# Interleaving loads and stores in one DMA ring, with a one-instruction row mean

## Chip, cores and metric

One core of a Trainium2 chip. The metric is the device time of one execution in microseconds (us); lower is better. Each version runs several times beside the kernel before on the same chip; medians are quoted. A ratio is computed as the mean time of one kernel's fast runs over the mean of the other's fast runs of the same rounds, so it isn't quite the ratio of the medians. "Same" means within 2%.

The profile knows these engines: DVE is VectorE, ACT ScalarE, POOL GpSimd and SP the engine that issues the transfers here. "DMA engines" are the 16 that move data. Besides the printed views I used the trace's packet records: one for each piece of a transfer (one partition's contiguous bytes) with its start and length. The records don't name the engine: figures per engine are sums divided by 16, or follow from one packet's end meeting the next one's start.

The "ring" is the queue's list of issued transfers. A transfer is "issued" when the instruction that queues it runs, and has "landed" when the profile reports it complete. Nearly all packets of one size took the same time: 2418 ns for 64 KiB (382 of 384 in the kernel before, within 1%), 1966 for 52 and 1815 for 48 (126 of 128 and 226 of 256 in the first profile of the changed kernel), 460 for 12 (all 128 in a3). Such packets are called undisturbed.

## The reference

```python
def reference(x, axis):           # x: 1024 x 4096 float32, axis = -1
    mean = np.mean(x, axis=axis, keepdims=True)
    return ((x - mean) ** 2).astype(np.float32)
```

16.78 MB in, 16.78 MB out. Each of the 128 partitions holds eight rows of 16 KiB.

## The kernel before

Two tiles of four rows each. All loads are issued at once, on one queue; each tile is stored when all its rows are done. Means are split between VectorE (rows 0 to 2) and ScalarE (row 3); ScalarE squares all but the last 1792 columns of row 2, which VectorE squares.

```python
for i in range(ntiles):                       # ntiles = 2, Q = 4 rows per tile
    x_tile = io.tile([P, Q * D], F32)
    cuts = [0, HEAD, Q * D] if i == 0 else [0, Q * D]      # HEAD = 512
    for lo, hi in zip(cuts, cuts[1:]):
        nc.sync.dma_start(out=x_tile[:, lo:hi], in_=x_t[i][:, lo:hi])
# ... cut: helpers for mean and square ...
for i in range(ntiles):
    row = [tiles[i][:, q * D:(q + 1) * D] for q in range(Q)]
    m3 = mean_on_act(row[3])
    m0 = mean_on_dve(row[0])
    square_on_act(row[3], m3)
    # ... cut: rows 1 and 2 alike, the end of row 2 squared on VectorE ...
    nc.sync.dma_start(out=out_t[i], in_=tiles[i])
```

Of the kernel before, what the change touches and what calls it, by code (L numbers as in the profile page):

```python
# [2 lines left out]

os.environ.setdefault("NEURON_RT_ULTRASERVER_MODE", "4")

# [4 lines left out]

F32 = mybir.dt.float32
ACT = mybir.ActivationFunctionType


@with_exitstack
def kernel(
    ctx: ExitStack,
    tc: tile.TileContext,
    x: bass.AP,
    axis: bass.AP,  # L20
    out: bass.AP,
):





    nc = tc.nc

    B, D = x.shape  # L30
    P = nc.NUM_PARTITIONS
    Q = 4
    HEAD = 512
    H = D * 9 // 16
    assert B % (P * Q) == 0
    ntiles = B // (P * Q)
    inv_d = 1.0 / float(D)

    x_t = x.rearrange("(p n q) d -> n p (q d)", p=P, q=Q)
    out_t = out.rearrange("(p n q) d -> n p (q d)", p=P, q=Q)  # L40

    io = ctx.enter_context(tc.tile_pool(name="io", bufs=ntiles))
    scratch = ctx.enter_context(tc.tile_pool(name="scratch", bufs=1))
    stats = ctx.enter_context(tc.tile_pool(name="stats", bufs=2 * ntiles * Q))

    tiles = []
    for i in range(ntiles):
        x_tile = io.tile([P, Q * D], F32)
        cuts = [0, HEAD, Q * D] if i == 0 else [0, Q * D]
        for lo, hi in zip(cuts, cuts[1:]):  # L50
            nc.sync.dma_start(out=x_tile[:, lo:hi], in_=x_t[i][:, lo:hi])  # L51
        tiles.append(x_tile)

    inorder = tc.keep_in_program_order

    def mean_on_act(row):
        copy = scratch.tile([P, D], F32)
        neg_mean = stats.tile([P, 1], F32)
        nc.scalar.activation(  # L59
            out=copy, in_=row, func=ACT.Identity, scale=-inv_d, accum_out=neg_mean  # L60
        )
        return neg_mean

    def mean_on_dve(row):
        neg_sum = stats.tile([P, 1], F32)
        neg_mean = stats.tile([P, 1], F32)
        inorder(nc.vector.reduce_sum(  # L67
            out=neg_sum, in_=row, axis=mybir.AxisListType.X, negate=True
        ))
        inorder(nc.vector.tensor_scalar_mul(out=neg_mean, in0=neg_sum, scalar1=inv_d))  # L70
        return neg_mean

    def square_on_act(part, neg_mean):
        inorder(nc.scalar.activation(  # L74
            out=part, in_=part, func=ACT.Square, bias=neg_mean, scale=1.0
        ))

    for i in range(ntiles):
        row = [tiles[i][:, q * D:(q + 1) * D] for q in range(Q)]
        m3 = mean_on_act(row[3])  # L80
        m0 = mean_on_dve(row[0])
        square_on_act(row[3], m3)
        m1 = mean_on_dve(row[1])
        square_on_act(row[0], m0)
        m2 = mean_on_dve(row[2])
        square_on_act(row[1], m1)
        square_on_act(row[2][:, :H], m2)
        back = row[2][:, H:]
        nc.vector.tensor_scalar_add(out=back, in0=back, scalar1=m2)  # L89
        nc.vector.tensor_mul(out=back, in0=back, in1=back)  # L90
        nc.sync.dma_start(out=out_t[i], in_=tiles[i])


# [1 line left out]
_INS = ['x', 'axis']  # L95
_OUTS = [((1024, 4096), 'float32')]

_NUMBERS = {'axis': -1}


# [26 lines left out]
```

## Time and profile before

| kernel before | |
|---|---|
| time, 6 runs | 83.28 us median (83.11 to 84.35) |
| span in the profile | 81.4 us |
| VectorE, ScalarE busy | 33.4, 34.7 us |
| DMA queue busy, as share of 16 engines | 95.9% |
| first store issued | 39.56 us |
| last load packets end, by engine (packet records) | 40.8 to 41.6 us |

A digit in the rows by slice is the busy share of one fortieth of the span, in tenths. The prediction below shows the lines of the engines, the queue, the compute groups and the stores. One more line matters later, from the list of DMA issues of the kernel before. Its last column is the time from issue to landing:

```profile
x_tile<-in_x_dram SPq DMA_DIRECT2D x1, 40.2
```

This is the second load, issued near 1.6 us behind the others and landed at 41.9.

### The profile page before, as it was taken

Reading aid. Unit: us, or ns where it says so; the run is one execution under the profiler, and the core shown is the slowest. Engines: PE = TensorE matmul, PEld = TensorE weight load, DVE = VectorE, ACT = ScalarE, POOL = GpSimd, SP = SyncE. Lnnn points to the kernel's source line nnn. Section 1 sums busy time; section 2 is a strip of 40 time slices with the busy share of each in tenths; the row PEclk is TensorE's granted clock in tenths of the full one; section 3 lists DMA queues with packets and bytes.
Section 4 is the critical chain, followed back from the end, with each engine's and each line's share of the span. In section 5 each row is a group of like instructions: output and inputs, shape, how many; then the busy total and the mean of one; then the engine's idle time right before and its main releaser. Section 6 shows DMA issues by size and latency. Waiting matters only on the chain.

```text
span 81.4 us, 83 instructions
## 1 busy us (share of the span) xinstructions
DVE 33.4 (41%) x16; ACT 34.7 (43%) x13; POOL 0.2 (0%) x4
## 2 busy tenths in 40 slices
DVE  0000000000089999999439999999900000000000
ACT  6000000000099999999339999999800000000000
POOL 0000000000000000000000000000000000000000
DMA  1999939999992999993899998399999199999290
GB/s 26 602 499 468 406 156 468 499 499 499 516 451 97 483 516 516 516 483 161 387 516 516 516 483 387 161 516 516 516 516 451 64 516 516 516 516 483 129 419 0
DMA packets 720, 33.55 MB, mean 412 GB/s; under 512 B 80, under 2 KB 80, under 8 KB 208
## 3 DMA queue, kind: packets, MB, share of 16 engines
q1 hardware_dynamic: 720, 33.55, 95.9%
HBM read 16.78 MB, written 16.78 MB: 412 GB/s over the span
## 4 chain that ended last, share of the span: by engine, by line
DMA 49%; DVE 21%; SPq 1%; issue 0%
DMA x_tile<-in_x_dram 49%; DVE neg_sum L67 16%; DVE x_tile L90 2%; DVE x_tile L89 1%; SPq L51 1%; DVE neg_mean L70 1%
## 5 line engine op out<-in xcount | busy, mean ns | idle before, releaser
L67 DVE TENSOR_REDUCE neg_sum<-x_tile 128x1 f32<-128x4096 f32 x6 | 26.5, 4412 | 25.0 <-DMA x_tile<-in_x_dram 25.0
L74 ACT ACTIVATE x_tile<-x_tile,neg_mean 128x4096 f32<-128x4096 f32 (+1 forms) x8 | 26.0, 3324 | 0.1
L59 ACT ACTIVATE copy<-x_tile 128x4096 f32<-128x4096 f32 x2 | 7.2, 3617 | 23.1 <-DMA x_tile<-in_x_dram 23.1
L90 DVE TENSOR_TENSOR x_tile<-x_tile 128x1792 f32<-128x1792 f32 x2 | 4.1, 2026 | 0.1
L89 DVE TENSOR_SCALAR x_tile<-x_tile,neg_mean 128x1792 f32<-128x1792 f32 x2 | 2.3, 1153 | 0.1
L59 ACT ACT_TABLE_LOAD x1 | 1.3, 1283 | 0.7 <-PEq L108 0.7
L70 DVE TENSOR_SCALAR neg_mean<-neg_sum 128x1 f32<-128x1 f32 x6 | 0.9, 154 | 0.2
L59 ACT ACTIVATION_READ_ACCUMULATOR copy<-x_tile 128x1 f32 x2 | 0.4, 186 | 0.0
L108 POOL MEMSET const-bfloat16-1.0<- 128x1 bf16 x1 | 0.1, 102 | 0.0
L108 POOL MEMSET const-uint8-127<- 128x1 uint8 x1 | 0.1, 101 | 0.0
L108 POOL MEMSET const-float32-0.0<- 128x1 f32 x1 | 0.1, 99 | 0.2 <-issue 0.2
L108 POOL MEMSET const-float32-1.0<- 128x1 f32 x1 | 0.1, 98 | 0.0
## 6 DMA issues: line engine op xcount, KB each, us to landing
x_tile<-in_x_dram SPq DMA_DIRECT2D x1, 7936.0 KB, 21.4
x_tile<-in_x_dram SPq DMA_DIRECT2D x1, 256.0 KB, 2.6
out_dram<-x_tile SPq DMA_DIRECT2D x2, 21.7
x_tile<-in_x_dram SPq DMA_DIRECT2D x1, 40.2
```

The lines of the kernel that those rows point to most:

```text
L51: nc.sync.dma_start(out=x_tile[:, lo:hi], in_=x_t[i][:, lo:hi])
L59: nc.scalar.activation(out=copy, in_=row, func=ACT.Identity, scale=-inv_d, accum_out=neg_mean)
L67: inorder(nc.vector.reduce_sum(out=neg_sum, in_=row, axis=mybir.AxisListType.X, negate=True))
L70: inorder(nc.vector.tensor_scalar_mul(out=neg_mean, in0=neg_sum, scalar1=inv_d))
L74: inorder(nc.scalar.activation(out=part, in_=part, func=ACT.Square, bias=neg_mean, scale=1.0))
L89: nc.vector.tensor_scalar_add(out=back, in0=back, scalar1=m2)
L90: nc.vector.tensor_mul(out=back, in0=back, in1=back)
L108: nc = _bacc.Bacc("TRN2", target_bir_lowering=False, num_devices=1)
```

## The change

Its intent: put the first store into the ring before the last piece of the loads, so that the ring alternates and results leave earlier, and cut compute with one VectorE instruction that adds a row's two halves, scales and sums them.

```diff
-    for i in range(ntiles):
-        x_tile = io.tile([P, Q * D], F32)
-        cuts = [0, HEAD, Q * D] if i == 0 else [0, Q * D]
-        ...
+    data = io.tile([P, ROWS * D], F32)
 ...
-        inorder(nc.vector.reduce_sum(
-            out=neg_sum, in_=row, axis=mybir.AxisListType.X, negate=True
-        ))
-        inorder(nc.vector.tensor_scalar_mul(out=neg_mean, in0=neg_sum, scalar1=inv_d))
+        inorder(nc.vector.tensor_tensor_reduce(
+            out=pairs, in0=row[:, :HALF], in1=row[:, HALF:],
+            scale=-inv_d, scalar=0.0, op0=ADD, op1=ADD, accum_out=neg_mean,
+        ))
 ...
+    load(0, 512)
+    load(512, 4 * D)
+    load(4 * D, 8 * D - 3 * D // 4)
+    for r in range(3):
+        compute(r)
+    store(0, 2)
+    load(8 * D - 3 * D // 4, 8 * D)
+    for r in range(3, 6):
+        compute(r)
+    store(3, 5)
+    for r in range(6, 8):
+        compute(r)
+    store(6, 7)
```

`load(lo, hi)` and `store(first, last)` are transfers on the same queue, in program order; `compute(r)` is the mean on VectorE and the whole square on ScalarE.

More of the change, by code (lines that the diff above doesn't have):

```diff
@@ L12 @@
 ACT = mybir.ActivationFunctionType
+ADD = mybir.AluOpType.add
 @with_exitstack
@@ L31 @@
     P = nc.NUM_PARTITIONS
-    Q = 4
-    HEAD = 512
-    H = D * 9 // 16
-    assert B % (P * Q) == 0
-    ntiles = B // (P * Q)
+    ROWS = B // P
+    HALF = D // 2
+    assert B == P * ROWS and ROWS == 8
     inv_d = 1.0 / float(D)
-    x_t = x.rearrange("(p n q) d -> n p (q d)", p=P, q=Q)
-    out_t = out.rearrange("(p n q) d -> n p (q d)", p=P, q=Q)
-    io = ctx.enter_context(tc.tile_pool(name="io", bufs=ntiles))
+    x_t = x.rearrange("(p r) d -> p (r d)", p=P)
+    out_t = out.rearrange("(p r) d -> p (r d)", p=P)
@@ L43 @@
+    io = ctx.enter_context(tc.tile_pool(name="io", bufs=1))
     scratch = ctx.enter_context(tc.tile_pool(name="scratch", bufs=1))
-    stats = ctx.enter_context(tc.tile_pool(name="stats", bufs=2 * ntiles * Q))
-    tiles = []
-    for i in range(ntiles):
-        x_tile = io.tile([P, Q * D], F32)
-        cuts = [0, HEAD, Q * D] if i == 0 else [0, Q * D]
-        for lo, hi in zip(cuts, cuts[1:]):
-            nc.sync.dma_start(out=x_tile[:, lo:hi], in_=x_t[i][:, lo:hi])
-        tiles.append(x_tile)
@@ L54 @@
-    inorder = tc.keep_in_program_order
-    def mean_on_act(row):
-        copy = scratch.tile([P, D], F32)
-        neg_mean = stats.tile([P, 1], F32)
-        nc.scalar.activation(
-            out=copy, in_=row, func=ACT.Identity, scale=-inv_d, accum_out=neg_mean
-        )
-        return neg_mean
-    def mean_on_dve(row):
-        neg_sum = stats.tile([P, 1], F32)
-        neg_mean = stats.tile([P, 1], F32)
-        inorder(nc.vector.reduce_sum(
-            out=neg_sum, in_=row, axis=mybir.AxisListType.X, negate=True
-        ))
-        inorder(nc.vector.tensor_scalar_mul(out=neg_mean, in0=neg_sum, scalar1=inv_d))
-        return neg_mean
@@ L73, in square_on_act, with load, store, compute @@
-    def square_on_act(part, neg_mean):
+    stats = ctx.enter_context(tc.tile_pool(name="stats", bufs=ROWS))
+    data = io.tile([P, ROWS * D], F32)
+    inorder = tc.keep_in_program_order
+    def load(lo, hi):
+        inorder(nc.sync.dma_start(out=data[:, lo:hi], in_=x_t[:, lo:hi]))
+    def store(first, last):
+        part = slice(first * D, (last + 1) * D)
+        inorder(nc.sync.dma_start(out=out_t[:, part], in_=data[:, part]))
+    def compute(r):
+        row = data[:, r * D:(r + 1) * D]
+        pairs = scratch.tile([P, HALF], F32)
+        neg_mean = stats.tile([P, 1], F32)
+        inorder(nc.vector.tensor_tensor_reduce(
+            out=pairs,
+            in0=row[:, :HALF],
+            in1=row[:, HALF:],
+            scale=-inv_d,
+            scalar=0.0,
+            op0=ADD,
+            op1=ADD,
+            accum_out=neg_mean,
+        ))
@@ L74, in square_on_act @@
         inorder(nc.scalar.activation(
-            out=part, in_=part, func=ACT.Square, bias=neg_mean, scale=1.0
+            out=row, in_=row, func=ACT.Square, bias=neg_mean, scale=1.0
         ))
-    for i in range(ntiles):
-        row = [tiles[i][:, q * D:(q + 1) * D] for q in range(Q)]
-        m3 = mean_on_act(row[3])
-        m0 = mean_on_dve(row[0])
-        square_on_act(row[3], m3)
-        m1 = mean_on_dve(row[1])
-        square_on_act(row[0], m0)
-        m2 = mean_on_dve(row[2])
-        square_on_act(row[1], m1)
-        square_on_act(row[2][:, :H], m2)
-        back = row[2][:, H:]
-        nc.vector.tensor_scalar_add(out=back, in0=back, scalar1=m2)
-        nc.vector.tensor_mul(out=back, in0=back, in1=back)
-        nc.sync.dma_start(out=out_t[i], in_=tiles[i])
+    load(0, 512)
```

## The prediction

> **What bounds the kernel now.** I read the page from the top. Its first two parts say that no compute engine is the limit and that the transfers are:
>
> ```profile
> DVE 33.4 (41%) x16; ACT 34.7 (43%) x13; POOL 0.2 (0%) x4
> ...
> DMA  1999939999992999993899998399999199999290
> ...
> q1 hardware_dynamic: 720, 33.55, 95.9%
> HBM read 16.78 MB, written 16.78 MB: 412 GB/s over the span
> ```
>
> VectorE and ScalarE work for about 40% of 81.4 us. The one DMA queue keeps all 16 DMA engines busy for 95.9% of the span, 78.1 us. The work in those 78.1 us is fixed by the reference: 33.55 MB, 2,097,152 bytes for each engine, so 2,097,152 / 78.1 us = 26.9 bytes per ns and engine. The isolated low digits in the DMA row come from how whole packets of 2.4 us fall into slices of 2.0 us: in the packet records of the trace each engine starts the next packet within some 5 to 10 ns of the one before, from the first packet at 1.74 us to the last end at 80.22 us. What is left of the span is 1.74 us ahead (the first issue at 0.73, a further 1.0 us until its first packet) and 1.1 us behind.
>
> The chain of work that ended last names DMA for only half of the span and then VectorE:
>
> ```profile
> 1.64 40.24 DMA x_tile<-in_x_dram
> ...
> 55.57 1.16 DVE x_tile L89
> ...
> 56.76 2.02 DVE x_tile L90
> ```
>
> This chain stops at 58.8 us, where the second store is issued, and does not follow it through the queue. It would mislead: shortening VectorE's part would only put that store into the ring sooner, behind a store that isn't done. The queue's own waits and the issues show this:
>
> ```profile
> 39.56 19.64 SPq L91 DMA_DIRECT2D out_dram<-x_tile  x2
> ...
> out_dram<-x_tile SPq DMA_DIRECT2D x2, 21.7
> ```
>
> Store 1 is issued at 39.56 us while the second load lands at 41.88 us; store 2 is issued at 58.9 us (39.56 + 19.64 less its own 0.35), store 1 lands at 39.56 + 21.7 = 61.3 us. Both stores are queued about 2.3 us before the ring reaches them, so no compute time is exposed at all. **The bound is one ring that is never empty**, and its length is bytes over rate.
>
> [...] a 65,536-byte packet took 2.418 us, 27.1 bytes per ns, times 16 is 433.7 GB/s. [...] on the single queue the packets of store 1 start at 41 us, when the load's end, although it was issued at 39.56. So the change can put work in another order in this ring but can't get it through sooner. [...]
>
> **The change part by part.**
>
> *Bytes.* The same 33.55 MB, one queue. Nothing to gain: 2,097,152 / 27.1 = 77.4 us per engine before and after.
>
> *Mean and square.* Away go six reductions of 4412 ns, six small scalings of 154 ns, two ScalarE means of 3617 ns and the two VectorE squares:
>
> ```profile
> L67 DVE TENSOR_REDUCE neg_sum<-x_tile 128x1 f32<-128x4096 f32 x6 | 26.5, 4412 | 25.0 <-DMA x_tile<-in_x_dram 25.0
> L59 ACT ACTIVATE copy<-x_tile 128x4096 f32<-128x4096 f32 x2 | 7.2, 3617 | 23.1 <-DMA x_tile<-in_x_dram 23.1
> L90 DVE TENSOR_TENSOR x_tile<-x_tile 128x1792 f32<-128x1792 f32 x2 | 4.1, 2026 | 0.1
> L89 DVE TENSOR_SCALAR x_tile<-x_tile,neg_mean 128x1792 f32<-128x1792 f32 x2 | 2.3, 1153 | 0.1
> L70 DVE TENSOR_SCALAR neg_mean<-neg_sum 128x1 f32<-128x1 f32 x6 | 0.9, 154 | 0.2
> ```
>
> In their place come eight add-and-sum instructions over two halves of 2048 columns. An estimate from L90: [...] about 0.1 us to write the sum out (ScalarE's accumulator read took 186 ns), so 2.4 us. VectorE then works 8 x 2.4 = 19 us instead of 33.4. ScalarE does eight full squares of 3.7 us, 29.6 us instead of 34.7. All of this lies beside the ring; by itself it is worth nothing.
>
> *When the first store reaches the ring.* Here the change can cost something. The two first loads are as before, so row 0 starts at 22.61 us as L67 did. Its mean ends at 25.0; three squares follow on ScalarE, which the trace shows starting 3.60 us apart (four, one of them 2.20 us long, took 13.01), so 2 x 3.60 + 3.70 = 10.9 and the last ends at 25.07 + 10.9 = 35.97. Issue at 36.03 us (L91 was issued 0.06 us after VectorE's end). First packet 1.0 us later, as at the start: 37.04 us. The third load is now 52 KiB per partition: the engines began it between 21.5 and 22.2 us, and eight packets of 53,248 / 27.1 = 1.965 us end at 37.2 to 37.9 us. The store comes **0.2 us ahead of the first engine that runs dry, 0.9 ahead of the last**. It should fit, but before the margin was 2.3 - 1.0 = 1.3 us; now it is nearly gone.
>
> *Later issues.* Store of rows 0 to 2: eight packets of 48 KiB per engine, 14.5 us, to about 52; the last 12 KiB, 3.6 us, to 55.7. Rows 4 and 5 land near 38.3, their squares end near 48.2: store of rows 3 to 5 is issued 7 us before it is needed. Row 7 lands near 56.4, takes 2.4 + 3.7, so the last store is issued near 62.7, while the one ahead runs to 70. Both hidden.
>
> *Ring overhead.* The ring has 7 transfers instead of 5, that is 56 instead of 40 packets per engine; a 2 KiB packet took 81 ns at best against 75.6 by rate, so about 5 ns each: 0.08 us. It changes direction three times (load to store, store to load, load to store) instead of once. Before, the packets after the switch began 2.49 to 2.62 us after the ones ahead, normally 2.41: 0.1 to 0.2 us per switch. Two more: about 0.2 us, partly taken up by slack between engines (they finish 0.54 us apart).
>
> *Sum:* 83.23 + 0.08 + about 0.1 = **83.4 us**, a change of 0.2%.
>
> **Rivals.** (1) *The add-and-sum runs at half rate*[...]: 4.3 + 0.1 us a row. The first mean ends 2.1 us later; ScalarE still follows 3.7 us behind, VectorE's pace of 4.4 now sets the third square: 22.61 + 3 x 4.4 + 3.7 + 0.1 = 39.6, first packet 40.6. The ring stands empty for 2.7 to 3.4 us and the time is about 86.3. [...] I give it 6%. (2) *A small hole at the first store*: a fixed cost of 0.3 to 0.8 us more in the new instruction, or a slower issue, empties the ring by about as much: 83.6 to 84.2. The 0.2 us margin speaks for it; I give it 30%. (3) *Less VectorE and ScalarE work shows as time*: the chain suggests VectorE's 21% matter. It would make 80 or less. Against it: both stores already wait in the ring; bytes at 433.7 GB/s leave only the ends of the span, 2.9 us, and the change touches neither. 1%. (4) *The mix of directions lets reads and writes overlap in the engines* and runs above 27.1 bytes per ns: the packets of both directions take the same 2.418 us[...]. 1%, about 82.
>
> **Range and chances.** The centre is 83.4. The low end, 83.0, is the run-to-run scatter below 83.2; the high end, 84.3, holds a hole of 0.9 us. Over 2% slower means above 84.9, a hole of 1.5 us or more: rival 1 and a bad case of rival 2, together 7%. Over 2% faster, below 81.6, needs rival 3 or more than rival 4: 1%. The rest, 92%, is the same.
>
> **What would show it.** In the changed profile: one queue at 95 to 96% of the span again, with 33.55 MB; VectorE near 19 us and ScalarE near 31 us with its table load; the add-and-sum near 2.3 us in the groups (4.4 would mean rival 1); the first store issued near 36.0 us; the DMA row near 37 us without a hole wider than a slice's scatter; stores 2 and 3 issued about 7 us before the ring comes to them. The prediction is wrong if the first store is issued after 37 us, if any later store is issued to an empty ring, if the switches of direction cost over 0.5 us each, or if the custom add-and-sum brings a start-up that holds back the first load.

## The result

The changed kernel took 84.48 us (median of 6, 84.03 to 87.23) against 83.28. The ratio of fast runs is 1.013, 95% interval 1.0098 to 1.0162. That is within 2%, as forecast, but above the predicted range of 83.0 to 84.3, and clear of noise. Two of the six runs were slow (87.23 and 85.36 us); the four fast ones took 84.03 to 84.52, with a median of 84.29, at the range's upper edge. Executions over 1.5% slower than the fastest of the same kernel are left out of the means.

The profile taken with it fell in a slow run (87.23 us), where in the packet records one DMA engine of the 16 ran about 1.5 us behind the others from the start. So I read the next profile of the same, unedited kernel, a fast run with a span of 82.6 us (run a1 below). First its engines, the DMA row and the groups that took the place of the old ones:

```profile
DVE 18.4 (22%) x16; ACT 30.4 (37%) x9; POOL 0.2 (0%) x4
...
DMA  1999974999999999999998889799899998799990
...
q1 hardware_dynamic: 1008, 33.55, 96.1%
HBM read 16.78 MB, written 16.78 MB: 406 GB/s over the span
...
L68 ACT ACTIVATE data<-data,neg_mean 128x4096 f32<-128x4096 f32 x8 | 29.1, 3698 | 10.8 <-DVE neg_mean L58 10.8
L58 DVE CUSTOM_DVE_ANT_0 pairs<-data 128x2048 f32<-128x2048 f32 x8 | 18.3, 2292 | 41.7 <-DMA data<-in_x_dram 41.5
...
L58 DVE DVE_READ_ACCUMULATOR2_ANT neg_mean<- 128x1 f32 x8 | 0.7, 83 | 0.0
```

VectorE's work fell by 15 us and ScalarE's by 4. The queue carries the same bytes and is busy for 96.1% of a span that is 1.2 us longer: 0.961 x 82.6 = 79.4 us against 0.959 x 81.4 = 78.1. So the time wasn't lost with an idle queue: **the same bytes kept the engines occupied 1.3 us longer**. The DMA row can't say which packets. The order of issues says when each store was ready. From the timeline of the same profile (start, duration, what):

```profile
35.93 0.35 SPq L52 DMA_DIRECT2D out_dram<-data  x1
36.32 0.43 SPq L48 DMA_DIRECT2D data<-in_x_dram  x1
...
48.06 16.12 SPq L52 DMA_DIRECT2D out_dram<-data  x2
```

And from its list of DMA issues:

```profile
data<-in_x_dram SPq DMA_DIRECT2D x1, 6656.0 KB, 36.6
...
data<-in_x_dram SPq DMA_DIRECT2D x1, 1536.0 KB, 21.3
```

The first store comes in time (35.93 us; the packets of the load ahead end at 37.2 to 37.9). The packet records put the loss in the middle: the load of the last 12 KiB, eight packets per engine that take 460 ns each when undisturbed, takes 0.9 us more than 8 x 460 ns in the mean over the engines. Of the last four packets of each engine, 64 in all, 42 took 500 to 1140 ns.

### The profile page after: what moved, and what is told of

It reads as the page before. It is cut to its first block, busy times and chain, and to the rows that moved or that the text cites. A ratio compares the mean times of both kernels' runs of the same rounds, so it can differ in the third digit from the quotient of the medians.

```text
span 85.5 us, 86 instructions
## 1 busy us (share of the span) xinstructions
DVE 18.4 (22%) x16; ACT 30.4 (36%) x9; POOL 0.2 (0%) x4
## 4 chain that ended last, share of the span: by engine, by line
DMA 53%; ACT 17%; DVE 5%; SPq 1%; issue 1%; DVEq 0%
DMA data<-in_x_dram 53%; ACT data L68 17%; DVE pairs L58 5%; SPq L48 0%; SPq L52 0%; DVEq L58 0%; DVE neg_mean L58 0%; DVEq L115 0%
## 5 line engine op out<-in xcount | busy, mean ns | idle before, releaser
L68 ACT ACTIVATE data<-data,neg_mean 128x4096 f32<-128x4096 f32 x8 | 29.1, 3699 | 12.1 <-DVE neg_mean L58 12.1
L58 DVE CUSTOM_DVE_ANT_0 pairs<-data 128x2048 f32<-128x2048 f32 x8 | 18.3, 2292 | 44.5 <-DMA data<-in_x_dram 44.3
L58 DVE DVE_READ_ACCUMULATOR2_ANT neg_mean<- 128x1 f32 x8 | 0.7, 82 | 0.0
```

The costliest lines, as they stand in the source:

```text
L58: inorder(nc.vector.tensor_tensor_reduce(out=pairs, in0=row[:, :HALF], in1=row[:, HALF:], scale=-inv_d, scalar=0.0, op0=ADD, op1=ADD, accu ...
L68: inorder(nc.scalar.activation(out=row, in_=row, func=ACT.Square, bias=neg_mean, scale=1.0))
```

## The experiments

I had these theories, in the order in which they came.

- **H**: the first store comes too late and the ring runs dry. (The prediction's second rival.)
- **S**: the ring's turn from store to load costs about 1 us.
- **P**: packets of 12 KiB are slow by themselves. **Q** is its successor: a short last load just ahead of a store, or the extra transfers, cost.
- **L**: a store that stands ready in the ring well before its turn slows the end of the load ahead of it; a store that comes just in time doesn't.
- **R** and **A**, two forms of L: under R the engines fetch ahead the waiting store's data, and the cost grows with the bytes there are to fetch; under A any waiting store does it.

Fifteen kernels ran, all with correct results, 4 to 6 runs each, on three chips. The table has the median, the ratio to the kernel before of the same call (its median lay between 82.99 and 83.02), and what the packet records say: by how much the packets of the load ahead of the store took longer than undisturbed ones, summed per engine and averaged over the 16.

| run | packets of the load ahead | store behind it issued, us | median, us | ratio | load packets longer by, us |
|---|---|---|---|---|---|
| a1 changed kernel | 12 KiB | 48.06 | 84.34 | 1.0161 | 0.90 |
| a2 | 12 KiB | 35.79 | 84.60 | 1.0183 | 1.14 |
| a3 | 52 KiB | 32.17 | 84.44 | 1.0176 | 1.31 |
| a4 | 64 KiB | 39.48 | 83.03 | 1.0004 | 0.02 |
| b1 | 64 KiB | 35.73 | 84.37 | 1.0172 | 1.24 |
| b2 | 12 KiB | 39.46 | 83.15 | 1.0017 | 0.00 |
| b3 | 12 KiB | 53.48 | 83.27 | 1.0032 | 0.02 |
| b4 | 64 KiB | 39.50 | 83.24 | 1.0020 | 0.03 |
| c1 | 64 KiB | 36.93 | 84.27 | 1.0148 | 1.34 |
| c2 | 64 KiB | 37.85 | 84.06 | 1.0146 | 1.04 |
| d3 | 64 KiB | 38.62 | 83.65 | 1.0071 | 0.64 |

In a4 the packets of both stores, equal in size, are in the sum. Runs c3, c4, d1 and d2 stand in their own sections.

### a1, a2, a3, a4: which part costs

a1 is the changed kernel once more.

> The changed kernel once more, unedited, because its one profile fell in a slow run. All theories: 84.0 to 84.6 us, 1.2 to 1.4% over the kernel before. Theory S (the ring's turn from store to load costs about 1.1 us): in a fast profile the first store is issued near 36.1 us and the ring has no hole near 37 us (under 0.3 us), while the last packet before the last load and that load's packets together take about 1 us longer than by rate. Theory H (the first store comes late to a ring run dry): the store is issued after 36.5 us and the engines stand idle 0.8 us or more around 37.5 us.

Measured: 84.34 us, and the profile shown above. The store was issued at 35.93 us and the first packets of the first store follow the last of the load with gaps of 2 to 3 ns. **H falls.**

a2 moves the 12 KiB load ahead of the first store, so that the ring turns only once:

```diff
     load(4 * D, 8 * D - 3 * D // 4)
+    load(8 * D - 3 * D // 4, 8 * D)
 ...
     store(0, 2)
-    load(8 * D - 3 * D // 4, 8 * D)
```

> The load of the last 12 KiB goes ahead of the first store, so the ring turns once, as before; everything else stays. Theory S: 83.2 to 83.4 us, the whole loss gone. Theory H: also 83.2 to 83.4, since the ring holds 3.6 us more work when the store comes. Theory P (packets of 12 KiB are slow by themselves, whatever stands beside them): 84.0 or more, nothing gained.

Measured: 84.60 us. Nothing was gained although the turn from store to load is gone, so **S falls**. P still stands.

a3 stores two rows first, and thereby earlier:

```diff
-    for r in range(3):
+    for r in range(2):
         compute(r)
-    store(0, 2)
+    store(0, 1)
     load(8 * D - 3 * D // 4, 8 * D)
-    for r in range(3, 6):
+    for r in range(2, 6):
         compute(r)
-    store(3, 5)
+    store(2, 5)
```

> The first store takes two rows and is issued 3.6 us earlier, near 32.4 us; the order load, store, load stays, with the same 12 KiB. Theory H: 83.2 to 83.5 us, since the store can't come late. Theory S: 84.1 to 84.5 us, the turn is still there. Theory P: 84.1 to 84.5 as well.

Measured: 84.44 us. But the loss has moved: here all 128 packets of 12 KiB took 460 ns, so **P falls**; now the load of 52 KiB ahead of the first store was slow, 37.8 us to landing where a1 had 36.6. From the list of DMA issues of a3:

```profile
data<-in_x_dram SPq DMA_DIRECT2D x1, 6656.0 KB, 37.8
data<-in_x_dram SPq DMA_DIRECT2D x1, 1536.0 KB, 20.3
```

In the packet records each engine's last 52 KiB packet took 3.0 to 3.6 us instead of 1.97.

a4 has the ring of the kernel before and the new compute:

```diff
-    load(4 * D, 8 * D - 3 * D // 4)
-    for r in range(3):
+    load(4 * D, 8 * D)
+    for r in range(4):
         compute(r)
-    store(0, 2)
-    load(8 * D - 3 * D // 4, 8 * D)
+    store(0, 3)
 ...                       # rows 4 to 7, then store(4, 7)
```

> The ring of the kernel before (three loads, two stores of 64 KiB per partition) with the changed kernel's mean and square alone. Theories S, H and P alike: 83.1 to 83.4 us, as before, for the compute part lies beside the ring. If the added instruction itself costs (a start-up, contention with the transfers): 84 us or more.

Measured: 83.03 us, ratio 1.0004 (0.9987 to 1.0021). The new mean costs nothing and gains nothing; the whole loss is in the ring.

What the slow transfers share is not their size. In a1, a2 and a3 a store had been issued 6 to 8 us before the load ahead of it would have ended undisturbed; where nothing was lost, a store came at most some 3 us ahead. That is theory L.

### b1, b2, b3, b4: early or just in time

b1 has whole loads (no 12 KiB piece) and only an early first store:

```diff
-    load(4 * D, 8 * D - 3 * D // 4)
+    load(4 * D, 8 * D)
 ...
     store(0, 2)
-    load(8 * D - 3 * D // 4, 8 * D)
```

> All loads first and whole (the last 64 KiB per partition, no 12 KiB load), then stores of 3, 3 and 2 rows. The ring turns once. The first store is issued near 35.9 us, some 6 us before the loads end. Theory L (a store that already stands in the ring more than some 3 us before its turn slows the last 50 to 60 KiB per engine of the load ahead of it, by about 1.2 us in all; one that comes later doesn't): 84.1 to 84.5 us, and the last one or two 64 KiB load packets take about 1.2 us longer in all. Theory Q (a short last load, 12 KiB packets just ahead of a store, or the extra transfers) : 83.0 to 83.3 us.

b4 is b1 with a needless square of 4096 columns on ScalarE ahead of row 2's, which holds the store back by 3.8 us (39.50 less 35.73); its result is used nowhere:

```diff
-    for r in range(3):
+    for r in range(2):
         compute(r)
+    spend(1, D)           # ScalarE: scratch = row 1 squared
+    compute(2)
     store(0, 2)
```

> As b1, with one needless square of 4096 columns ahead of row 2's, so that the first store is issued near 39.5 us, 2.4 us before the loads end, as in the kernel before. Theory L: 83.0 to 83.3 us, 1.2 less than b1. Theory Q: the same as b1, whatever that is.

Measured: b1 84.37 us, b4 83.24. The issues of the stores in the timeline (start of the first, stretch to the end of the last issue), first b1's, then b4's:

```profile
35.73 24.78 SPq L52 DMA_DIRECT2D out_dram<-data  x3
```

```profile
39.50 19.76 SPq L52 DMA_DIRECT2D out_dram<-data  x3
```

And the second load in the lists of DMA issues, b1's, then b4's:

```profile
data<-in_x_dram SPq DMA_DIRECT2D x1, 41.6
```

```profile
data<-in_x_dram SPq DMA_DIRECT2D x1, 40.3
```

The load in b1 is issued at the same moment and moves the same bytes, but lands 1.3 us later, because a store was waiting behind it. The packet records agree: one packet per engine, the last, took 3.4 to 4.0 us in b1 and 2.42 in b4 (2.70 on one engine).

b2 takes a2's loads, 12 KiB piece and all, with a first store of four rows, which therefore is issued at 39.46 us:

```diff
-    for r in range(3):     # against a2
+    for r in range(4):
         compute(r)
-    store(0, 2)
+    store(0, 3)
```

> The loads of a2, with the 12 KiB load last among them, but the first store takes four rows and so is issued 3.6 us later, near 39.5 us, about 2 us before the loads end. Theory L: 83.0 to 83.3 us, and the 12 KiB packets take 460 ns each. Theory Q: 84.1 to 84.6 us as a2.

Measured: 83.15 us against a2's 84.60; the 12 KiB packets took 460 ns. From the lists of DMA issues of a2, then of b2, the 12 KiB load:

```profile
data<-in_x_dram SPq DMA_DIRECT2D x1, 1536.0 KB, 41.0
```

```profile
data<-in_x_dram SPq DMA_DIRECT2D x1, 1536.0 KB, 39.8
```

**Q falls.**

b3 is the changed kernel with its second store held back by needless work:

```diff
-    for r in range(3, 6):
-        compute(r)
+    for r in range(3, 5):
+        compute(r)
+    spend(4, D)
+    spend(4, D // 2)
+    compute(5)
     store(3, 5)
```

> The changed kernel with two needless squares (4096 and 2048 columns, about 5.5 us of ScalarE's time, results unused) ahead of row 5's, so that the second store is issued near 53.6 us and not at 48.1, some 2 us before the 12 KiB load ends. Theory L: more work, less time: 83.0 to 83.4 us. Theory Q and every theory of switches: 84.2 us or more. If 83.5 to 84.0, a part of the loss is at the turn from store to load.

Measured: 83.27 us. **With 5.56 us more ScalarE work the changed kernel runs 1.07 us faster.** From b3's timeline, the needless squares and the issue of the held store:

```profile
44.30 5.56 ACT L75 ACTIVATE spent<-data 128x4096 f32<-128x4096 f32 x2
...
53.48 9.60 SPq L52 DMA_DIRECT2D out_dram<-data  x2
```

From its list of DMA issues, the 12 KiB load:

```profile
data<-in_x_dram SPq DMA_DIRECT2D x1, 1536.0 KB, 20.4
```

The 12 KiB load lands 20.4 us after its issue instead of 21.3 in a1, and its packets are back at 463 ns in the mean. All four b runs came out as L said. The needless work isn't what helps: a4 and b2 issue their store late without any.

The packet records also say what is left in b3. The last packet of the first store, just ahead of the 12 KiB load, took longer, by 0.26 us per engine in the mean (in a1 by 0.26 as well). So the turn from store to load had a small cost of its own there; in a3 it had none (0.00), and what sets it stays open.

### c1, c2, d3: how late is late enough

b1 with 1024, 2048 and 3072 columns of needless square: `spend(1, D // 4)`, `spend(1, D // 2)` and `spend(1, 3 * D // 4)` ahead of `compute(2)`.

> b1 with a needless square of 1024 columns ahead of row 2's: the first store is issued near 36.8 us, 1.0 later than in b1 and 2.7 earlier than in b4. If the cost is all or nothing, set by whether the store stands in the ring when the last load packet begins (38.4 to 38.9 us[...]): 84.2 to 84.5 us, as b1. If it grows with the lead: 84.0 us or less.

> As c1 with 2048 columns: issue near 37.7 us[...], while the last load packets begin at 38.4 to 38.9. All or nothing by engine: some engines show a last load packet of 3.4 us or more and others 2.42 us, and the time, which the slowest engines set, lies between 83.3 and 84.3 us. Growing with the lead: near 83.6 us and all last packets alike, about 2.9 us.

> b4 with a needless square of 3072 columns: issue near 38.7 us, between c2 (37.85, cost 1.1) and b4 (39.5, cost 0.2). Threshold at the start of the last load packet (38.5 to 39.0): no cost, 83.0 to 83.3 us. Cost that falls linearly with issue from c2 to b4: about 83.6 us.

Measured: 84.27, 84.06 and 83.65 us with issue at 36.93, 37.85 and 38.62. The second load in the lists of DMA issues of c1 (whose profile was its slowest run, 84.74 us), c2 and d3:

```profile
data<-in_x_dram SPq DMA_DIRECT2D x1, 41.8
```

```profile
data<-in_x_dram SPq DMA_DIRECT2D x1, 41.1
```

```profile
data<-in_x_dram SPq DMA_DIRECT2D x1, 40.7
```

For c2 both forms missed: every engine's last packet was longer, by "all or nothing by engine" some should not have been, and all took 3.2 to 3.7 us, more than the 2.9 of "growing with the lead". d3's linear form hit (83.6 expected). Taken with b1 and b4 the cost is about flat for a store issued at 37 us or earlier (1.24 and 1.34 us) and then falls: 1.04 at 37.85 us, 0.64 at 38.62, 0.03 at 39.50. That is from 4.5 to 2 us before this load's undisturbed end at 41.5. The limit isn't one number for all loads: d3's store, 2.9 us ahead, still cost 0.64 us, while in a3 the second store was issued 3.2 us before the end of the 12 KiB load and cost nothing.

### c3: the store in a second ring

b1 with its first store issued from ScalarE's queue:

```diff
-    store(0, 2)
+    inorder(nc.scalar.dma_start(out=out_t[:, :3 * D], in_=data[:, :3 * D]))
```

> b1 with its first store issued from ScalarE's queue instead, still near 35.9 us, so it doesn't stand behind the loads but beside them in a second ring. If the loss belongs to one ring's order (the read ahead for the store getting in front of the load's end): 83.1 to 83.4 us. If loads and stores in flight together cost whatever their ring: 84.3 us or more, and load packets beside the store take well over 2.42 us.

Measured: 85.22 us, ratio 1.0268: worse than b1. From its list of DMA issues:

```profile
out_dram<-data ACTq DMA_DIRECT2D x1, 6144.0 KB, 21.4
...
data<-in_x_dram SPq DMA_DIRECT2D x1, 43.6
```

The load's packets grew by 1.03 us per engine, about as in b1, so **the loss isn't tied to one ring's order**. Being in a second ring didn't bring the store forward, either: it was issued at 36.44 us, and its first packets began at 42.42 to 43.03, when the load's last had ended. So this run, too, tests a waiting store and not one that moves beside the load. The 0.85 us over b1 I don't explain: in this profile the first 62 KiB packets were slower too (2.95 us in the mean against 2.58 in b1), and the first packet per engine of the second store, which is in the other ring than the first store, took 2.55 us in the mean instead of 1.815.

### d1, d2: does the waiting store's size matter

b4, whose main store comes just in time, but with a first piece of row 0 stored by itself near 29 us: 2 KiB per partition (d1) or 16 KiB (d2).

```diff
     compute(0)
+    store_cols(0, 512)             # d2: store_cols(0, D)
     compute(1)
     spend(1, D)
     compute(2)
-    store(0, 2)
+    store_cols(512, 3 * D)         # d2: store_cols(D, 3 * D)
```

> b4 (main store issued near 39.5 us, which cost nothing), but the first 2 KiB per partition of row 0 are stored by a transfer of their own issued near 28.7 us, 13 us before the loads end. Theory R (the engines fetch the waiting store's data ahead and this gets in the way of the load's end; the cost grows with the bytes that are there to fetch): 83.1 to 83.4 us, under 0.15 over b4. Theory A (any store waiting behind the load, however small, slows the load's last packets): 84.2 to 84.5 us.

> As d1, but the early transfer is the whole row 0, 16 KiB per partition, issued near 28.7 us. Theory R: between d1 and b1, the load's end late by 0.3 to 0.9 us, time 83.5 to 84.0 us; if only a few packets are fetched ahead, up to 84.3. Theory A: 84.2 to 84.5 us, the same as d1.

Measured: 84.00 us (ratio 1.0126) and 84.82 us (1.0212, 84.31 to 85.21; whether it is over 2% slower is unclear). The early store and the main one in the timelines, d1's and d2's:

```profile
29.10 11.19 SPq L78 DMA_DIRECT2D out_dram<-data  x2
```

```profile
28.81 11.19 SPq L78 DMA_DIRECT2D out_dram<-data  x2
```

The load packets grew by 0.46 us per engine in d1 and by 1.05 in d2, against 0.03 in b4. With 32 KiB waiting it was 1.31 (a3), with 48 KiB 0.90 to 1.34 (a1, a2, b1, c1). So the load's end is held up by less when only 2 KiB of store data wait, which A denies, and from 16 KiB up no clear growth shows. That is R's order, but neither time fits R's sizes: d1 is 0.76 us over b4 and d2 1.58, of which 0.43 and 1.02 are the load. d1's profile was its slowest run, 84.81 us, with one engine behind (without that engine the growth is 0.41). The remaining 0.3 to 0.6 us, in rings with one more transfer each, stays open.

No run beat the kernel before. c4 tried, with a4's ring without the 2 KiB head load:

```diff
-    load(0, 512)          # against a4
-    load(512, 4 * D)
+    load(0, 4 * D)
     load(4 * D, 8 * D)
```

> The candidate for a faster version: the kernel before's two whole loads and two stores of 64 KiB per partition, the new mean, and no 2 KiB head load (no work ever started on it). Issue of the first store near 39.4 us, 2.3 us before the loads end, so no loss by theory L. 128 fewer packets and one issue less ahead: 82.6 to 83.0 us; if the head load doesn't cost, 83.0 to 83.1.

Measured: 83.20 us, ratio 1.0020. The head load costs nothing; the expected gain was a miss.

## Why the prediction was wrong

**The bound** was right: one ring that isn't empty. **Compute beside the ring** was right: the add-and-sum took 2292 ns and its read-out 83 ns (a1), together the 2.4 us forecast, and a4 shows that it is worth nothing (ratio 1.0004). The 2.4 us, and rival 1's half rate and 4.3 us a row, were my estimates, not shown by a trace then; scaled by columns from L90, whose 1792 took 2026 ns, 2048 columns would be 2.32 us. **When the first store reaches the ring** was right: issue at 35.93 us (36.03), no hole; its rivals 1 and 2, half rate and a late store, didn't occur, and neither did 3 or 4. Its comparison of margins was misread: the 1.3 us that it gives for the kernel before run to the load's landing (41.88 us), the 0.2 to 0.9 us for the changed kernel to the packets' ends. To the packets' ends (40.8 to 41.6 us) the kernel before had 0.3 to 1.0 us, so the change hardly cut this margin.

**The step that failed** is in "Later issues": "store of rows 3 to 5 is issued 7 us before it is needed ... Both hidden." It took a store in the queue before its turn for free, and treated only lateness as a risk. The runs show the reverse: the second store was issued 8 us before the end of the 12 KiB load ahead of it, and that load's last packets paid for it. Held back to 2.7 us ahead, the same store gave 83.27 us (b3): 1.07 of the 1.32 us that a1 lost. The kernel before had hidden this from me. Its only store behind a load was issued 2 us ahead of the load's last packet end, just in time by accident (one engine stood idle for 0.2 us before its first store packet), and I read this margin as a safety to be enlarged, not as a limit. None of the signs of being wrong that the prediction lists names this: the stores were issued early, as it asked.

That "same" came true is luck: it allowed 0.2 us, the loss was 1.3 us, and this just stayed within 2%. The range's upper end, which the fast runs reach, was held for a hole of 0.9 us that never came.

**Ring overhead** was sized at 0.2 us for packets and turns. What is left in b3, 0.26 us by medians, has this size, and the store's last packets ahead of the 12 KiB load account for as much. But b4, with one turn and no such packets, shows 0.23 as well, so the runs don't say what a turn costs. The reading behind the estimate was off, too: of the spacings at the switch in the kernel before, only the two largest are 2.49 and 2.62 us (the second is the idle engine); the other 14 are 2.42 to 2.47.

**Why a waiting store slows a load** isn't shown. Shown is where and when: it happens at the end of the load, in the last packet of 52 or 64 KiB of each engine (3.0 to 3.6 us in a3, 3.4 to 4.0 in b1) or the last four of 12 KiB (42 of 64 took 500 to 1140 ns in a1); it depends on when the store is issued (1.24 us in b1, 0.03 in b4), not on the number of turns (one turn in a2: 1.14), the packet size (0.90 to 1.34 from 12 to 64 KiB) or the ring (c3: 1.03); it was smaller with 2 KiB per partition waiting (0.46 us) than with 16 to 48 KiB (0.90 to 1.34). That the engines fetch the waiting store's data ahead (theory R) is my guess; no run shows such a fetch. If it were so, nothing was gained later: the store's own packets took 1815 ns each in b1, as undisturbed ones do. An estimate: at 27.1 bytes per ns (65,536 bytes in 2418 ns) the 1.24 us lost in b1 would be some 34 KB fetched ahead per engine. A transfer has 128 packets, eight per engine, so in d1 16 KiB per engine waited, at most 0.6 us by the same estimate against 0.46 measured, and in d2 128 KiB, more than the 34 KB; this would be why no clear growth shows from 16 KiB up. The guess doesn't say why c3's store, in a second ring, cost as much, and a3's free store 3.2 us ahead shows that it lacks something.

## What to carry to other kernels

In a kernel bound by transfers, ask of a store not only whether it is issued before the ring runs dry, but also how long it waits there behind a load: here 2 us ahead was free (a4, b4: 0.02 and 0.03 us), 2.7 to 3.2 us free behind 12 KiB packets (b3, a3) but not behind 64 KiB ones (d3, 2.9 us: 0.64 us lost), and with 16 KiB or more per partition waiting 4.5 us or more cost 0.9 to 1.3 us (a1 to a3, b1, c1, d2). A queue that is busy to 96% can still lose time (a1: 96.1% busy, 1.32 us over the kernel before), so compare how long the same load takes to land, version against version, before looking at the engines. Work off the critical path can save time by holding the next transfer back: b1 has 3.6 us less ScalarE work than b4, issues its store 3.8 us earlier and takes 1.13 us longer. a4 and b3 separate the two effects, by changing the work alone and by holding the transfer back alone.
